# Feed-forward chunks: the order of 512-column and 256-column products on TensorE

## The chip, the cores and the metric

The kernel runs on one core of a Trainium2 chip. Its engines are TensorE (PE in the profile, with its weight loads as PEld), VectorE (DVE), ScalarE (ACT), GpSimd (POOL) and SyncE (SP, which issues nearly all DMAs here). The metric is the device time of one launch in microseconds, lower is better. Three runs of the kernel before took 1203.28, 1199.79 and 1201.71 us, median 1201.71 us.

## The reference, cut to what matters

Two decoder layers over 256 tokens of width 1024. Each layer has two feed-forward parts (SwiGLU), with a token mixer and a cross-attention between them. The change touches the feed-forward parts alone:

```python
def swiglu_ffn(x, w_gu, w_down):
    gate, up = jnp.split(x @ w_gu, 2, axis=-1)
    return (jax.nn.silu(gate) * up) @ w_down
# D_MODEL = 1024, D_FF = 2816: w_gu is 1024 x 5632, w_down 2816 x 1024, all float32
# per layer: x += 1/2 swiglu(rms_norm(x)); mixer; cross-attention; x += 1/2 swiglu(rms_norm(x))
```

So there are four feed-forward parts in the program, each with a gate-and-up product and a down product.

## The kernel before, in words

Every float32 operand is split in two float32r parts, a high part (the rounded value) and a low part (the rest). A product is then three products: high by high, high by low, low by high. The helper `weights` brings one weight tile of 128 x 1024 by DMA into one of four `raw` buffers; for the gate-and-up weights that is two DMAs of 256 KB (line 171). ScalarE casts the tile to its high part `wh` (line 175) and VectorE subtracts to get the low part `wl` (line 177). There are ten buffers each for `wh` and `wl`, and a `raw` buffer is free again when its `wl` is done.

The gate-and-up product of one feed-forward part is done in eleven chunks of 256 features. A chunk uses four weight tiles; tile i holds the rows of k = 2i and 2i + 1, the 256 gate columns and the 256 up columns. Weights are stationary here and the activations stream: `xs` holds, per k, the high part of 2 x 128 tokens and the low part of 2 x 128 tokens, four runs of 128 columns in all. A product with `wh` therefore streams 512 columns (high and low part of x, line 323) into the two halves of a PSUM bank, and a product with `wl` streams 256 columns (the high part of x alone, line 324) and adds to the first half. The helper `ws_wide` does this for one half of a chunk (g = 0 gate, g = 1 up): two banks (b), and for each bank eight k, the 512-column product and the 256-column product in turn. A chunk has 4 banks and 32 such pairs. When a bank is done, ScalarE copies its second half out (line 327) and VectorE adds the first half to it (line 328). Then come the Silu (line 416), the product with the up half (line 418) and the split of the result into two parts (lines 190 and 191, tile `big`).

In the first feed-forward part chunk 0 is done in another way (lines 305 and 182 to 184, streams of 256 columns), and chunks 1 to 10 with `ws_wide`. In the other three, chunks 0 and 1 are done by tokens (lines 182 to 184, streams of 512 columns), and chunks 2 to 10 with `ws_wide`; while chunk 2 runs, two transposes of line 397 come in between. That makes 10 + 3 x 9 = 37 wide chunks, 1184 pairs. The down product `project` follows with streams of 512 columns (lines 182 to 184).

PSUM has six rotating banks for these products. Engines work through their instructions in the order that the scheduler wrote; TensorE's order is that of the source, with the delayed pieces (`later`, `tick`) put in where their due time on the planner's clock has passed. The DMA queue is SyncE's; it issues a weight tile when a `raw` buffer is free.

Of the kernel before, what the change touches and what calls it, by code (L numbers as in the profile page):

```python
# [18 lines left out]
P = 128  # L19
S = 256  # L20
D = 1024
NK = D // P
# [16 lines left out]
def kernel(  # L39
# [33 lines left out]
    nc = tc.nc  # L73
# [18 lines left out]
    def later(delay, fn, tag=None):  # L92
        serial[0] += 1
        heapq.heappush(heap, (clock[0] + delay, serial[0], tag, fn))

    def dispatch():
        due, _, _, fn = heapq.heappop(heap)
        clock[0] = max(clock[0], due)
        busy[0] = True
        fn()  # L100
        busy[0] = False

    def tick(ns):
        clock[0] += ns
        if heap and not busy[0] and heap[0][0] <= clock[0]:
            dispatch()

    def need(tag):
        while any(e[2] == tag for e in heap):
            dispatch()  # L110

    def flush():
        while heap:
            dispatch()
# [27 lines left out]
    xs = const.tile([P, 2, 2, NK, P], F32R, name="xs")  # L142
    xh, xl = xs[:, 0], xs[:, 1]
# [3 lines left out]
    def psum():  # L147
        return mm.tile([P, 512], F32, name="mm")

    def tps():  # L150
        return tp.tile([P, 512], F32, name="tp")

    def slot(dt=F32):
        return big.tile([P, 1024], dt, name="big")

    def work(dt=F32):
        return wk.tile([P, 512], dt, name="wk")
# [4 lines left out]
    def blocks(ap, n=P):  # L162
        return ap.rearrange("p (a b) -> p a b", b=n)


    def weights(src, r=None, kept=False):
        if r is None:
            r = raw.tile([P, 1024], F32, name="raw")
        if len(src.shape) == 4:
            for g in range(2):  # L170
                nc.sync.dma_start(r.rearrange("p (k g n) -> p k g n", g=2, n=src.shape[3])[:, :, g, :], src[:, :, g, :])
        else:
            (kept_load if kept else nc.sync.dma_start)(r if len(src.shape) == 2 else blocks(r, src.shape[2]), src)
        wh = wsp.tile([P, 1024], F32R, name="wh")
        nc.scalar.copy(wh, r)  # L175
        wl = wsp.tile([P, 1024], F32R, name="wl")
        nc.vector.tensor_tensor(wl, r, f32(wh), op=ALU.subtract)  # L177
        return wh, wl

    def mm3(ps, a, b, start, stop):  # L180

        nc.tensor.matmul(ps, lhsT=a[0], rhs=b[0], start=start, stop=False)  # L182
        nc.tensor.matmul(ps, lhsT=a[0], rhs=b[1], start=False, stop=False)  # L183
        nc.tensor.matmul(ps, lhsT=a[1], rhs=b[0], start=False, stop=stop)  # L184

    def cols(w, o, n):
        return w[0][:, o:o + n], w[1][:, o:o + n]

    def split_to(dh, dl, src):
        nc.scalar.copy(dh, src)  # L190
        nc.vector.tensor_tensor(dl, src, f32(dh), op=ALU.subtract)  # L191
# [45 lines left out]
    def announce(vec, kept=False):  # L237
        upcoming["gain"] = None if vec is None else load_gain(vec, kept)
# [21 lines left out]
    def xparts(t, k):  # L260
        return xh[:, t, k, :], xl[:, t, k, :]
# [49 lines left out]
                mm3(ps[:, b * 256:(b + 1) * 256], cols(w[k // per], o, P), xboth(k), k == 0, k == NK - 1)  # L311
                tick(330)

    def ws_wide(w, g):


        part, out = work(), work()
        for b in range(2):
            ps = psum()
            for k in range(NK):  # L320
                o = (k % 2) * 512 + g * 256 + b * P
                wh, wl = cols(w[k // 2], o, P)
                nc.tensor.matmul(ps, lhsT=wh, rhs=xs[:, :, :, k, :], start=k == 0, stop=False)  # L323
                nc.tensor.matmul(ps[:, 0:256], lhsT=wl, rhs=xh[:, :, k, :], start=False, stop=k == NK - 1)  # L324
                tick(347)
            bs = slice(b * 256, (b + 1) * 256)
            nc.scalar.copy(part[:, bs], ps[:, 256:512])  # L327
            nc.vector.tensor_tensor(out[:, bs], ps[:, 0:256], part[:, bs], op=ALU.add)  # L328
        return out


    def start(load):


        et = mybir.EngineType
        with tc.manual_schedule(engines={et.Pool, et.DVE, et.Activation, et.PE}):
            upcoming["gain"] = [psum(), psum()]
            for c in range(2):
                nc.tensor.matmul(upcoming["gain"][c], lhsT=ones[0:1, 0:P], rhs=row[0:1, c * 512:(c + 1) * 512],
                                 start=True, stop=True)  # L340
            busy_ps = tps()
            for i in range(2):
                nc.tensor.matmul(busy_ps, lhsT=filler[:, 0:P], rhs=filler, start=i == 0, stop=i == 1)
            r0 = raw.tile([P, 1024], F32, name="raw")
            nc.vector.tensor_copy(r0[:, 0:1], xres[0][:, D - 1:D])
            for t in range(2):
                for c in range(2):
                    x_updated(t, c)
                clock[0] += 3000.0
            upcoming["starting"] = True  # L350
            need("x0")
            first = load(0, r0)
            need("x1")
            rest = load(1, None)
            upcoming["starting"] = False
            return first, rest

    def ffn(w_gu, w_down, next_vec, first=False):
        wv = w_gu.rearrange("(k p) n -> p k n", p=P)
        wgu = w_gu.rearrange("(k p) (g n) -> p k g n", p=P, g=2)  # L360
        hts = []

        def load_chunk(c):

            return [weights(wgu[:, 2 * i:2 * i + 2, :, c * 256:(c + 1) * 256]) for i in range(4)]

        def hslot(c):
            if c % 2 == 0:
                hts.append((slot(F32R), slot(F32R)))
            return [blocks(h[:, (c % 2) * 512:(c % 2) * 512 + 512], 256) for h in hts[c // 2]]  # L370

        ws = hs = None
        if first:
            f, r = start(lambda i, r: [weights(wv[:, 0:4, 0:256], r, kept=True)] if i == 0 else
                         [weights(wv[:, 4 * (n % 2):4 * (n % 2) + 4, (n // 2) * DFF:(n // 2) * DFF + 256],
                                 kept=True)
                          for n in range(1, 4)])
            ws = [[[f[0], r[0]], r[1:]]]
        else:
            need("x0")  # L380
            ws = [load_chunk(0), load_chunk(1)]
            hs = [hslot(0), hslot(1)]
        for t in range(2):
            need(f"x{t}")
            for c in range(0 if first else 2):
                ps = psum()
                for k in range(NK):
                    mm3(ps, xparts(t, k), cols(ws[c][k // 2], (k % 2) * 512, 512), k == 0, k == NK - 1)
                    tick(650)
                h = work()  # L390
                nc.scalar.activation(h[:, 0:256], ps[:, 0:256], AF.Silu)
                nc.vector.tensor_tensor(h[:, 256:512], ps[:, 256:512], h[:, 0:256], op=ALU.mult)

                def to_features(t=t, c=c, h=h):
                    pst = tps()
                    for b in range(2):
                        nc.tensor.transpose(pst[:, b * P:(b + 1) * P], h[:, 256 + b * P:256 + (b + 1) * P], ident)
                    split_to(hs[c][0][:, :, t * P:(t + 1) * P], hs[c][1][:, :, t * P:(t + 1) * P],
                             blocks(pst[:, 0:256]))
                later(LAG['silu'], to_features)  # L400
        if not first:
            announce(next_vec)
        for c in range(0 if first else 2, NF // 2):
            w = ws[0] if first and c == 0 else load_chunk(c)
            if first and c == 2:
                announce(next_vec, kept=True)
            if first and c == 0:
                pg = psum()
                ws_blocks(pg, w[0], 0, 4, by_pass=True)
                pu = psum()  # L410
                ws_blocks(pu, w[1], 0, 4)
            else:
                pg = ws_wide(w, 0)
                pu = ws_wide(w, 1)
            s = work()
            nc.scalar.activation(s, pg, AF.Silu)
            h = work()
            nc.vector.tensor_tensor(h, pu, s, op=ALU.mult)
            dh, dl = hslot(c)
            split_to(dh, dl, blocks(h, 256))  # L420
        flush()

        def hparts(t, k):
            o = (k % 4) * 256 + t * P
            return hts[k // 4][0][:, o:o + P], hts[k // 4][1][:, o:o + P]

        project(lambda k: w_down[k * P:(k + 1) * P, :], hparts, add_to_x(0.5), nk=NF)
# [626 lines left out]
```

## Time and profile before

| what | value |
|---|---|
| median of three runs | 1201.71 us (1199.79 to 1203.28) |
| profiled execution, its own time | 1202.92 us |
| span in the profile | 1201.2 us |
| PE busy | 1189.3 us (99%) |
| PEld busy | 998.7 us (83%) |
| DVE busy | 775.1 us (65%) |
| ACT busy | 646.5 us (54%) |
| DMA queue, share of 16 engines' span | 55.4% |

The span runs from the first to the last instruction in the profile; the execution's own time is 1.7 us longer. The duration of a matmul in the profile is longer than the distance to the next one's start, because matmuls overlap; what a product costs in a stream is read from the starts of neighbouring rows, not from its duration.

### The profile page before, as it was taken

How to read it: one execution, taken by the hardware profiler on the slowest of the kernel's cores; microseconds unless marked ns; L12 is line 12 of the kernel's file. 1: busy time of each engine (PE TensorE's matmuls, PEld its weight loads, DVE VectorE, ACT ScalarE, POOL GpSimd, SP SyncE). 2: the span in 40 equal slices, each digit the busy share in tenths (PEclk: the TensorE clock that was granted, in tenths of full speed). 3: DMA queues.
4: the chain of work that ended last, by engine and by line, in shares of the span. 5: the costliest groups of instructions: out<-in, count | busy, mean ns of one | idle time of the engine just before them, and what ended most of it. 6: DMA issues, size and time to landing. Idle time of an engine off the chain costs nothing.

```text
span 1201.2 us, 16964 instructions
## 1 busy us (share of the span) xinstructions
PE 1189.3 (99%) x6320; PEld 998.7 (83%) x6320; DVE 775.1 (65%) x1026; ACT 646.5 (54%) x1080; POOL 63.9 (5%) x123
## 2 busy tenths in 40 slices
PE   8999999999999999999999999999999999999998
PEld 7888888986788888888888888888777888888887
DVE  6766645696777676665375765376786676667651
ACT  6656534665565466555265564265764564655540
POOL 1000000200110000000000000032000100000000
PEclk9999999999999999999999999999999999999999
DMA  8865674731454485666376657445753645665560
GB/s 253 255 195 172 218 223 131 258 105 53 145 167 144 153 266 172 191 209 210 108 250 189 193 181 274 141 158 167 230 169 121 210 143 160 202 205 188 182 192 35
DMA packets 136756, 216.70 MB, mean 180 GB/s; under 512 B 10337, under 2 KB 104161, under 8 KB 136674
## 3 DMA queue, kind: packets, MB, share of 16 engines
q1 hardware_dynamic: 136674, 215.63, 55.4%
q8 instruction: 49, 0.80, 0.3%
q14 instruction: 33, 0.27, 0.1%
HBM read 214.54 MB, written 1.05 MB: 179 GB/s over the span
## 4 chain that ended last, share of the span: by engine, by line
PE 93%; DVE 3%; DMA 2%; ACT 1%; issue 1%; POOL 0%; SPq 0%; ACTq 0%; POOLq 0%; DVEq 0%
PE mm L323 23%; PE mm L182 17%; PE mm L184 17%; PE mm L183 17%; PE mm L324 12%; PE tp L212 3%; PE mm L496 1%; DVE wl L177 1%; DMA raw<-in_xa_w_o_dram 1%; DMA raw<-in_ffn_w_gu_dram 1%; ACT wh L175 1%; PE mm L305 1%; PE mm L841 1%; DVE big L191 0%; PE mm L705 0%
## 5 line engine op out<-in xcount | busy, mean ns | idle before, releaser
L177 DVE TENSOR_TENSOR wl<-raw,wh 128x1024 fp32r<-128x1024 f32 x386 | 463.9, 1220 | 145.4 <-ACT wh L175 142.5
L175 ACT CAST wh<-raw 128x1024 fp32r<-128x1024 f32 x386 | 394.3, 1051 | 156.9 <-PE mm L184 78.7
L323 PE MATMUL mm<-xs,wh 128*128 128x512 f32 x1184 | 413.7, 394 | 0.0
L324 PE MATMUL mm<-xs,wl 128*128 128x256 f32 x1184 | 331.8, 280 | 0.0
L323 PEld LDWEIGHTS mm<-xs,wh 128*128 128x128 f32 x1184 | 221.7, 187 | 50.3
L324 PEld LDWEIGHTS mm<-xs,wl 128*128 128x128 f32 x1184 | 223.8, 189 | 0.0
L182 PE MATMUL mm<-wh,big 128*128 128x512 f32 x480 | 191.3, 399 | 0.3 <-DVE wk L713 0.3
L184 PE MATMUL mm<-wh,big 128*128 128x512 f32 x480 | 188.4, 392 | 0.0
L183 PE MATMUL mm<-wl,big 128*128 128x512 f32 x480 | 188.2, 392 | 0.0
L182 PE MATMUL mm<-wh,xs 128*128 128x512 f32 (+1 forms) x432 | 171.7, 398 | 0.0
L184 PE MATMUL mm<-wh,xs 128*128 128x512 f32 (+1 forms) x432 | 167.1, 387 | 0.0
L183 PE MATMUL mm<-wl,xs 128*128 128x512 f32 (+1 forms) x432 | 167.0, 386 | 0.0
L327 ACT COPY wk<-mm 128x256 f32<-128x256 f32 x148 | 55.0, 372 | 147.1 <-PE mm L324 146.7
L328 DVE TENSOR_TENSOR wk<-mm,wk 128x256 f32<-128x256 f32 x148 | 62.1, 421 | 94.7 <-ACT wk L327 94.7
L182 PEld LDWEIGHTS mm<-wh,big 128*128 128x128 f32 x480 | 90.5, 188 | 20.3 <-issue 2.4
L184 PEld LDWEIGHTS mm<-wh,big 128*128 128x128 f32 x480 | 90.4, 188 | 19.3 <-issue 0.3
L183 PEld LDWEIGHTS mm<-wl,big 128*128 128x128 f32 x480 | 90.6, 189 | 17.4 <-issue 0.2
L184 PEld LDWEIGHTS mm<-wh,xs 128*128 128x128 f32 x432 | 81.1, 188 | 16.9 <-issue 0.2
L182 PEld LDWEIGHTS mm<-wh,xs 128*128 128x128 f32 x432 | 81.3, 188 | 15.0 <-issue 0.5
L183 PEld LDWEIGHTS mm<-wl,xs 128*128 128x128 f32 x432 | 81.4, 188 | 14.5 <-issue 0.2
L212 PE MATMUL tp<-ident,wk 128*128 128x128 f32 x352 | 52.9, 274 | 2.4 <-DVE wk L452 0.8
L212 PEld LDWEIGHTS tp<-ident,wk 128*128 128x128 f32 x352 | 42.1, 140 | 14.2 <-issue 2.3
(148 smaller groups left out, 921.6 us busy)
## 6 DMA issues: line engine op xcount, KB each, us to landing
raw<-in_ffn_w_gu_dram SPq DMA_DIRECT2D x344, 256.0 KB, 4.2
raw<-in_ffn_w_down_dram SPq DMA_DIRECT2D x88, 512.0 KB, 4.5
raw<-in_xa_w_kv_dram SPq DMA_DIRECT2D x32, 512.0 KB, 5.4
raw<-in_od_w_in_dram SPq DMA_DIRECT2D x24, 512.0 KB, 4.5
raw<-in_ev_w_in_dram SPq DMA_DIRECT2D x18, 512.0 KB, 4.7
raw<-in_xa_w_q_dram SPq DMA_DIRECT2D x16, 512.0 KB, 4.2
raw<-in_xa_w_o_dram SPq DMA_DIRECT2D x16, 512.0 KB, 4.4
raw<-in_ev_w_out_dram SPq DMA_DIRECT2D x8, 512.0 KB, 4.1
```

Of the source, the lines that this page charges most:

```text
L175: nc.scalar.copy(wh, r)
L177: nc.vector.tensor_tensor(wl, r, f32(wh), op=ALU.subtract)
L182: nc.tensor.matmul(ps, lhsT=a[0], rhs=b[0], start=start, stop=False)
L183: nc.tensor.matmul(ps, lhsT=a[0], rhs=b[1], start=False, stop=False)
L184: nc.tensor.matmul(ps, lhsT=a[1], rhs=b[0], start=False, stop=stop)
L212: nc.tensor.transpose(ps[:, b * P:(b + 1) * P], src[:, b * P:(b + 1) * P], ident)
L305: nc.tensor.matmul(ps[:, b * 256:(b + 1) * 256], lhsT=w[k // per][x][:, o:o + P], rhs=xboth(k)[y], start=i == 0 and k == 0, stop=i == 2 an ...
L323: nc.tensor.matmul(ps, lhsT=wh, rhs=xs[:, :, :, k, :], start=k == 0, stop=False)
L324: nc.tensor.matmul(ps[:, 0:256], lhsT=wl, rhs=xh[:, :, k, :], start=False, stop=k == NK - 1)
L327: nc.scalar.copy(part[:, bs], ps[:, 256:512])
L328: nc.vector.tensor_tensor(out[:, bs], ps[:, 0:256], part[:, bs], op=ALU.add)
L496: nc.tensor.matmul(dst(h)[rows], lhsT=lhs(h), rhs=rhs(h), start=first, stop=last)
```

## The change

`ws_wide`, called twice per chunk, becomes `ws_chunk`, called once. It does the 32 products of 512 columns of a chunk first, over four banks, and then the 32 products of 256 columns over the same four banks. The instructions are the same in number and kind; the copies and adds that empty a bank now follow that bank's last 256-column product, in the second part of the chunk.

```diff
-    def ws_wide(w, g):
-        part, out = work(), work()
-        for b in range(2):
-            ps = psum()
+    def ws_chunk(w):
+        pair, outs = [(g, b) for g in range(2) for b in range(2)], []
+        banks = []
+        for g, b in pair:
+            banks.append(psum())
             for k in range(NK):
                 o = (k % 2) * 512 + g * 256 + b * P
-                wh, wl = cols(w[k // 2], o, P)
-                nc.tensor.matmul(ps, lhsT=wh, rhs=xs[:, :, :, k, :], start=k == 0, stop=False)
-                nc.tensor.matmul(ps[:, 0:256], lhsT=wl, rhs=xh[:, :, k, :], start=False, stop=k == NK - 1)
-                tick(347)
+                nc.tensor.matmul(banks[-1], lhsT=w[k // 2][0][:, o:o + P], rhs=xs[:, :, :, k, :],
+                                 start=k == 0, stop=False)
+                tick(227)
+        for (g, b), ps in zip(pair, banks):
+            for k in range(NK):
+                o = (k % 2) * 512 + g * 256 + b * P
+                nc.tensor.matmul(ps[:, 0:256], lhsT=w[k // 2][1][:, o:o + P], rhs=xh[:, :, k, :],
+                                 start=False, stop=k == NK - 1)
+                tick(120)
+            if b == 0:
+                part, out = work(), work()
+                outs.append(out)
             bs = slice(b * 256, (b + 1) * 256)
             nc.scalar.copy(part[:, bs], ps[:, 256:512])
             nc.vector.tensor_tensor(out[:, bs], ps[:, 0:256], part[:, bs], op=ALU.add)
-        return out
+        return outs
...
-                pg = ws_wide(w, 0)
-                pu = ws_wide(w, 1)
+                pg, pu = ws_chunk(w)
```

On TensorE, where chunk 1 of the first feed-forward part begins, this stood before (`mm` is a PSUM bank, `xs` the activations, lines 182 to 184 the end of chunk 0):

```order
58 L182 MATMUL mm<-xs,wh 128x256
59 L183 MATMUL mm<-xs,wh 128x256
60 L184 MATMUL mm<-xs,wl 128x256
61 L323 MATMUL mm<-xs,wh 128x512
62 L324 MATMUL mm<-xs,wl 128x256
63 L323 MATMUL mm<-xs,wh 128x512
```

and so on, 32 times in turn per chunk. Now this stands there, with the whole of chunk 1 in its last two rows:

```order
58 L182 MATMUL mm<-xs,wh 128x256
59 L183 MATMUL mm<-xs,wh 128x256
60 L184 MATMUL mm<-xs,wl 128x256
61 L324 MATMUL mm<-xs,wh 128x512 x32
62 L330 MATMUL mm<-xs,wl 128x256 x32
```

Products of one size now stand 32 in a row and all four banks of the chunk stay open until its last third. No other instruction of TensorE has moved.

On VectorE, in chunk 2 of the same part, this stood before (`wl` is a low part being made for a later chunk, line 328 the add that empties a bank, line 418 the product with the up half, line 191 the split; numbers tell buffers apart):

```order
37 L191 TENSOR_TENSOR big_304<-wk_417,big_303 128x512
38 L328 TENSOR_TENSOR wk_452<-mm_453,wk_451 128x256
39 L328 TENSOR_TENSOR wk_452<-mm_472,wk_451 128x256
40 L328 TENSOR_TENSOR wk_492<-mm_493,wk_491 128x256
41 L177 TENSOR_TENSOR wl_672<-raw_667,wh_670 128x1024
42 L177 TENSOR_TENSOR wl_679<-raw_674,wh_677 128x1024
43 L328 TENSOR_TENSOR wk_492<-mm_512,wk_491 128x256
44 L177 TENSOR_TENSOR wl_774<-raw_769,wh_772 128x1024
45 L418 TENSOR_TENSOR wk_533<-wk_492,wk_531 128x512
```

and this stands there now:

```order
38 L338 TENSOR_TENSOR wk_496<-mm_451,wk_495 128x256
39 L338 TENSOR_TENSOR wk_496<-mm_460,wk_495 128x256
40 L177 TENSOR_TENSOR wl_672<-raw_667,wh_670 128x1024
41 L338 TENSOR_TENSOR wk_518<-mm_469,wk_517 128x256
42 L338 TENSOR_TENSOR wk_518<-mm_478,wk_517 128x256
43 L177 TENSOR_TENSOR wl_679<-raw_674,wh_677 128x1024
44 L427 TENSOR_TENSOR wk_533<-wk_518,wk_531 128x512
45 L177 TENSOR_TENSOR wl_774<-raw_769,wh_772 128x1024
46 L191 TENSOR_TENSOR big_536<-wk_533,big_535 128x512
47 L177 TENSOR_TENSOR wl_781<-raw_776,wh_779 128x1024
```

The four adds of a chunk now stand together, with one low part between the second and the third, and the other three low parts of the chunk's time behind them. ScalarE's order has moved in the same way: three casts, the copies of banks 0 and 1, one cast, the copies of banks 2 and 3, the Silu.

## Rows read from the trace of the kernel before

**Rows 1.** Page: busy time, share and instructions; granted clock in 40 slices.
```profile
PE 1189.3 (99%) x6320; PEld 998.7 (83%) x6320; DVE 775.1 (65%) x1026; ACT 646.5 (54%) x1080; POOL 63.9 (5%) x123
...
PEclk9999999999999999999999999999999999999999
```

**Rows 2.** Page: the chain that ended last, by engine and by line.
```profile
PE 93%; DVE 3%; DMA 2%; ACT 1%; issue 1%; POOL 0%; SPq 0%; ACTq 0%; POOLq 0%; DVEq 0%
PE mm L323 23%; PE mm L182 17%; PE mm L184 17%; PE mm L183 17%; PE mm L324 12%; PE tp L212 3%; PE mm L496 1%; DVE wl L177 1%; DMA raw<-in_xa_w_o_dram 1%; DMA raw<-in_ffn_w_gu_dram 1%; ACT wh L175 1%; PE mm L305 1%; PE mm L841 1%; DVE big L191 0%; PE mm L705 0%
```

**Rows 3.** Page: costliest groups (xcount, busy us, mean ns, idle before).
```profile
L177 DVE TENSOR_TENSOR wl<-raw,wh 128x1024 fp32r<-128x1024 f32 x386 | 463.9, 1220 | 145.4 <-ACT wh L175 142.5
L175 ACT CAST wh<-raw 128x1024 fp32r<-128x1024 f32 x386 | 394.3, 1051 | 156.9 <-PE mm L184 78.7
L323 PE MATMUL mm<-xs,wh 128*128 128x512 f32 x1184 | 413.7, 394 | 0.0
L324 PE MATMUL mm<-xs,wl 128*128 128x256 f32 x1184 | 331.8, 280 | 0.0
...
L327 ACT COPY wk<-mm 128x256 f32<-128x256 f32 x148 | 55.0, 372 | 147.1 <-PE mm L324 146.7
L328 DVE TENSOR_TENSOR wk<-mm,wk 128x256 f32<-128x256 f32 x148 | 62.1, 421 | 94.7 <-ACT wk L327 94.7
```

**Rows 4.** Windows, line 323 alone: us, PE busy (x), PEld busy (x), PEclk, DMA share, GB/s.
```profile
26.27:139.33 113.06, 113.06 (x320) 60.01 (x320) 1.00 0.65 208
448.60:543.20 94.60, 94.59 (x273) 51.03 (x273) 1.00 0.59 188
632.90:727.50 94.60, 94.50 (x274) 51.05 (x273) 1.00 0.59 187
1042.70:1137.30 94.60, 94.53 (x273) 51.05 (x273) 1.00 0.58 187
```

**Rows 5.** Windows, PE alone: us, PE busy (x), PEclk, DMA share, GB/s.
```profile
20.75:26.15 5.40, 5.40 (x47) 1.00 0.94 299
1142.07:1179.47 37.40, 37.40 (x167) 1.00 0.46 150
443.08:448.47 5.39, 5.39 (x33) 1.00 0.83 266
```

**Rows 6.** Timeline, PE, 512 to 256 to 512 columns (start us, us).
```profile
199.89 0.39 PE L184 MATMUL mm<-wh,big 128*128 128x512 f32 x1
200.12 0.28 PE L182 MATMUL mm<-wh,xs 128*128 128x256 f32 x1
...
202.99 0.40 PE L182 MATMUL mm<-wh,xs 128*128 128x512 f32 x1
203.22 0.40 PE L183 MATMUL mm<-wl,xs 128*128 128x512 f32 x1
...
204.15 0.39 PE L184 MATMUL mm<-wh,xs 128*128 128x512 f32 x1
```

**Rows 7.** Timeline, PE, a wide chunk of the second feed-forward part.
```profile
507.63 0.39 PE L323 MATMUL mm<-xs,wh 128*128 128x512 f32 x1
507.86 0.28 PE L324 MATMUL mm<-xs,wl 128*128 128x256 f32 x1
507.98 0.39 PE L323 MATMUL mm<-xs,wh 128*128 128x512 f32 x1
```

**Rows 8.** Timeline, one chunk: ACT, then DVE, with idle time before.
```profile
80.98 1.98 ACT L175 CAST wh<-raw 128x1024 fp32r<-128x1024 f32 x2
...
88.66 0.37 ACT L327 COPY wk<-mm 128x256 f32<-128x256 f32 x1 [1.52 <-PE mm L324]
91.53 0.37 ACT L327 COPY wk<-mm 128x256 f32<-128x256 f32 x1 [2.50 <-PE mm L324]
...
82.05 2.36 DVE L177 TENSOR_TENSOR wl<-raw,wh 128x1024 fp32r<-128x1024 f32 x2 [1.04 <-ACT wh L175]
85.80 0.69 DVE L418 TENSOR_TENSOR wk<-wk 128x512 f32<-128x512 f32 x1
...
87.87 0.68 DVE L191 TENSOR_TENSOR big<-wk,big 128x512 fp32r<-128x512 f32 x1
```

**Rows 9.** Issue of one weight tile on SP; DMA issues: xcount, KB each, us to landing.
```profile
72.00 0.88 SPq L171 DMA_DIRECT2D raw<-in_ffn_w_gu_dram  x2
...
raw<-in_ffn_w_gu_dram SPq DMA_DIRECT2D x344, 256.0 KB, 4.2
...
raw<-in_ffn_w_gu_dram SPq DMA_DIRECT2D x4, 512.0 KB, 6.9
```

## The prediction

> **What bounds the kernel now.** I read the page from the top. TensorE is busy 99% of the span, at the full clock (2.4 GHz, the granted share is at 9 or more tenths) in every slice [rows 1], and the chain of waits that ended last is 93% TensorE, 35% in the two lines that the change reorders [rows 2]. So the wide chunks are paid for at the pace at which TensorE starts products, and the only direct question is what 32 wide and 32 narrow products cost in turn and what they cost in two blocks. The mean durations of the groups (394 and 280 ns, [rows 3]) don't tell, since matmuls overlap. I took stretches and divided them by the number of starts.
>
> In turn, the kernel before shows two paces for the same instructions. In the first feed-forward part 320 pairs took 113.06 us, 353.3 ns a pair; in the other three, 273 pairs took 94.60 us, 346.5 ns (one window cuts so that it counts 274) [rows 4]. Among the latter I count only what follows the last transpose of line 397. The 15 pairs of chunk 2 before it took 5.39 us [rows 5]; at 346.5 ns they would take 5.20, so 0.19 us is lost there. A start right after transposes is late once; that part I put at 0.09 us and leave it as it is, and 0.10 is the slow pace (15 x 6.7 ns).
>
> In blocks, the nearest streams of one size are: 256 columns alone, the same activations and weights of the same kind, 45 steps in 5.40 us, 120.0 ns; 512 columns alone, in the down product, 165 steps in 37.40 us, 226.7 ns [rows 5]. Their sum is 346.7 ns. So the quick pace in turn is already the sum of the two streams, and the slow one is 6.7 ns above it. What the change can win is the slow pace, where it rules: 320 pairs of the first part, 45 in the others.
>
> **The change part by part.** TensorE's instructions keep their number: 1184 wide and 1184 narrow products with their weight loads.
>
> The blocks. A chunk is 32 x 226.7 + 32 x 120.0 ns = 11.09 us.
>
> The seams. A place that goes from wide to 24 narrow and back stands in the trace: from the last wide start at 199.89 to the sixth wide start after the narrow ones, at 204.15, are 4.26 us [rows 6]. The streams' paces give 0.227 + 24 x 0.120 + 5 x 0.2267 = 4.24. So two seams cost 0.02 us; the five wide starts behind the narrow stream come 0.232 us apart, near the slow pace, and then the pace is quick again. A chunk is thus 11.11 us.
>
> The sum. First part: 10 chunks x (32 x 0.3533 = 11.306, less 11.113) = 1.93 us less. Other parts: 27 chunks x (11.113 less 32 x 0.3465 = 11.088) = 0.68 more, and 3 x 0.10 less. In all 1.55 us less, on the profiled execution's 1202.92 us: 1201.4 us. That execution lies 1.2 us above the median of the runs, and I carry the saving over to the median: 1200.2 us.
>
> In the Trainium skill, "TensorE: Matmul & The Clock Gate", section Back-to-back issue gap, a warm product alone is given as its columns over 2.4 GHz and about 2.5 ns, here 216 and 109 ns. By it each size has one price, whatever its neighbour, and the change would be worth nothing. The two paces of one instruction pair in this trace (353.3 and 346.5 ns) are both above the 325 that it gives, and they differ: the trace does not agree.
>
> The emptying of banks. Four copies (0.372 us) and four adds (0.421 us) per chunk stay, but come at its end. A bank is needed again after the two spare ones: bank 0 is full 32 x 0.2267 + 8 x 0.12 = 8.2 us into the chunk and is needed 16 x 0.2267 = 3.6 us into the next, so 6.5 us later, of which copy and add take 0.8. That leaves 5.7 us in which waits on ScalarE are free. Before, ScalarE sat idle in front of these copies for 147 us in all [rows 3], 1.5 and 2.5 us at a time [rows 8]; it waited for TensorE, not the other way. I cost the move at nothing under that cover.
>
> The weights. The low parts of a chunk are freed only in its last 0.8 us now, and VectorE makes the new ones in the order one, then three behind the Silu of the chunk, with 0.69 us of other work between. The new round is: the last low part frees a raw buffer; SP's two issues (0.88 us, the second about 0.4 in) and 4.2 us to landing [rows 9], 4.6; the cast 1.05; copies of banks 2 and 3, 0.74; the add 0.42; then low part, product, low part, split, low part, 3 x 1.22 + 2 x 0.69 = 5.04 [rows 3, 8]. That is 11.85, less some 0.1 where neighbours on an engine overlap (two casts take 1.98 us and two low parts 2.36, [rows 8]), six times, so about 11.3 us against a chunk of 11.11. The round would slip 0.2 us per chunk, 2 us in ten chunks, out of 5.7. It stays hidden on these numbers, without much to spare. Products themselves have their weights a chunk or more ahead.
>
> **The rivals.**
>
> *Emptying of banks falls behind (slower).* The same round decides from a landing about 0.4 us over the 4.2, since a slip of 0.6 per chunk uses the 5.7 us in ten chunks. From then on TensorE waits at the third bank of each chunk. With landings 0.6 us longer the slip is 0.8, the cover lasts 7 chunks, and 3 chunks of the first part and 2 of each other pay: 9 x 0.8 = 7.2 us, less 1.55: 1207.4. For it: there are landings of 6.9 us in this trace, if of tiles in one piece [rows 9], and at the start of the first part the DMAs run at 208 GB/s over the whole part. Against it: the issues will come further apart (about 1.9 us) than they do now.
>
> *The wide block stays slow (slower).* The wide products read four runs of 128 columns, those of the down product one run of 512; no stream of the former alone is in the trace. If the five slow starts of [rows 6] go on through all 32, a chunk is 32 x (0.3533 - 0.120) + 3.84 = 11.306: nothing is won in the first part, and 27 x 0.218 less 0.3 = 5.6 us are lost: 1207.3. Against it: the quick pace in turn has room for no more than 226.7 ns for such a product, if the narrow one takes its 120.
>
> *Narrow products have been cheap in turn.* The starts in turn are 0.23 us from wide to narrow and 0.12 back [rows 7]. If a wide product really takes 0.230 and the narrow one less than 0.120 because its weight load is hidden under a wide one, blocks cost 350 ns a pair: 1.06 us less in the first part and 27 x 0.112 - 0.3 = 2.7 more: 1203.4. The Trainium skill, in the same page's section LDWEIGHTS, puts a load of 128 columns at their number over 1.2 GHz, 107 ns, as long as 256 streamed columns; no run here times a load alone.
>
> *The slow pace is no matter of order.* Then the first part stays at 353 ns a pair or the runs change between paces by themselves; the three runs differ by 3.5 us as it is. Nothing changes: 1201.7. If, the other way, the runs without profile have the slow pace in all parts, the gain is 37 x 0.193 = 7.1 us: 1194.6; the profiled one, above the median, has it in one part of four.
>
> **How the numbers follow.** My forecast has 0.50, the banks 0.18, the wide block 0.10, the narrow products 0.08, no change 0.09, the larger gain 0.05. What a measurement of this kernel can tell from no change is about 0.3%, 3.6 us. The forecast, the narrow products and no change lie within it; Of the forecast I give 0.07 to a saving over that bound, should the seams be cheaper and the slow pace more common than one profile shows; of the banks' case 0.03 to a loss below it. Faster 0.05 + 0.07 = 0.12, slower 0.15 + 0.10 = 0.25, same 0.63. The likeliest case alone reaches from 1198.5 to 1202. The range takes in both slower cases and a part of the larger gain: 1197 to 1208.5.
>
> **What would show it.** In the profile after: wide products in the chunks start 226 to 228 ns apart but for some five at the head of a block, narrow ones 120; a chunk takes 11.1 us in all four parts, and the first part's ten chunks end about 1.9 us earlier after their start. Rows of TensorE at the head of the third bank have no idle time in front, and ScalarE still waits for TensorE at the copies. I am wrong if gaps stand in front of the third wide bank, growing from chunk to chunk, if the wide blocks hold 233 ns, or if the first part has not changed its pace.

## The result: slower by 1.4%

The changed kernel took 1218.33 us (median of 4 runs, 1217.26 to 1222.16), the kernel before 1201.58 us beside it: a ratio of 1.0143, 95% interval 1.0122 to 1.0164. The forecast was 1200.2 us. The profiled execution of the changed kernel took 1219.17 us, its span is 1217.1 us, 15.9 more than before. In its profile the 512-column products are line 324, the 256-column ones line 330, the copies that empty a bank line 337 and the adds line 338.

The page of the changed kernel, busy times, then the chain that ended last by engine and by line; they answer to [rows 1, 2]:

```profile
PE 1193.1 (98%) x6320; PEld 999.6 (82%) x6320; DVE 768.8 (63%) x1026; ACT 645.8 (53%) x1080; POOL 63.9 (5%) x123
...
PE 62%; DVE 15%; DMA 13%; issue 6%; ACT 3%; SPq 1%; POOL 0%; ACTq 0%; DVEq 0%; POOLq 0%
PE mm L182 18%; PE mm L184 17%; PE mm L183 17%; DMA raw<-in_ffn_w_gu_dram 8%; DVE wl L177 7%; DMA raw<-in_ffn_w_down_dram 5%; DVE wk L338 4%; PE mm L324 3%; PE tp L212 3%; DVE wk L427 2%; ACT wh L175 1%; PE mm L505 1%; ACT wk L337 1%; PE mm
```

The share of busy time has hardly moved. The chain has: TensorE fell from 93% to 62% of it, and where lines 323 and 324 held 35%, the weights' DMA, the low parts and the adds now stand between TensorE's pieces.

The groups of the same page, which answer to [rows 3] (times, busy us and mean ns, idle before and what ended it), and the waits of the whole program (us, times, longest):

```profile
L175 ACT CAST wh<-raw 128x1024 fp32r<-128x1024 f32 x386 | 401.4, 1052 | 264.9 <-DMA raw<-in_ffn_w_gu_dram 96.2
...
L338 DVE TENSOR_TENSOR wk<-mm,wk 128x256 f32<-128x256 f32 x148 | 55.9, 417 | 161.7 <-ACT wk L337 161.6
...
raw<-in_ffn_w_gu_dram SPq DMA_DIRECT2D x344, 256.0 KB, 4.0
```

```profile
DVE wk L338 <- ACT wk L337: 161.6, 40, 4.9
...
PE mm L182 <- DVE wk L338: 9.0, 4, 2.5
```

Before, ScalarE's idle time stood in front of the copies and TensorE ended it (147 us). Now no such row is left for the copies. More idle time stands in front of the casts (264.9 us against 156.9), and the gate-and-up DMAs end 96.2 us of it (29.4 before); the adds wait up to 4.9 us for a copy, and four times, once per feed-forward part, TensorE waits 2.1 to 2.5 us for an add at the head of the down product.

The pace is as forecast. Windows of line 324 alone over the first wide chunk, then of line 330 in it (us, PE busy, PEld busy, clock, DMA share, GB/s); they answer to [rows 4]:

```profile
24.16:31.42 7.26, 7.26 (x32) 5.82 (x32) 1.00 0.84 263
...
31.43:35.26 3.83, 3.82 (x32) 3.78 (x31) 1.00 1.09 365
```

A wide product costs 7.26/32 = 0.227 us, a narrow one 0.120. What was not forecast stands in whole chunks. Windows of TensorE from the start of one wide chunk to the next (us, PE busy; the difference is idle time, as far as it outlasts the tail of the product before), first part, then the second:

```profile
46.39:57.50 11.11, 11.11 (x67) 1.00 0.52 161
68.65:80.65 12.00, 11.45 (x67) 1.00 0.55 167
80.65:92.59 11.94, 11.40 (x67) 1.00 0.60 189
92.59:103.95 11.36, 11.36 (x66) 1.00 0.59 167
103.95:116.11 12.16, 11.42 (x67) 1.00 0.61 195
116.11:127.35 11.24, 11.24 (x66) 1.00 0.53 169
...
513.55:525.22 11.67, 11.42 (x67) 1.00 0.61 187
```

The first four chunks take the 11.11 us of the forecast, the next five 58.70 us, 11.74 on the mean. TensorE waits there at the third bank, behind 16 of the 32 wide products; in the first of these chunks:

```profile
73.01 3.96 PE L324 MATMUL mm<-xs,wh 128*128 128x512 f32 x16 [0.55 <-DVE wk L338]
```

The two traces, laid side by side at the same instructions of TensorE, give the whole difference:

| where | us, after less before |
|---|---|
| up to the first wide chunk (loading of x and chunk 0, which the change doesn't touch) | -2.11 |
| wide chunks, pace and seams: first part -1.93, others +0.33 | -1.60 |
| wide chunks, waits at the third bank: parts one to four 3.77, 1.34, 1.06, 0 | +6.17 |
| down product, wait at its third bank: 2.36, 2.70, 2.48, 2.35 | +9.89 |
| down product of parts one and two, half clock behind that wait: 1.74, 1.76 | +3.50 |
| everything else | +0.04 |
| sum | +15.89 |

The first row stands ahead of all that the change touches: TensorE came to its full pace later in the trace of before, where four 256-column products of chunk 0 still take 1.22 us at 13.5 us; in that of after four take 0.74 at 12.5. Without this row the change costs 18.0 us here. "Everything else" is -0.43 and +0.47 between the parts.

**The round that is longer than a chunk.** ScalarE, then VectorE in a chunk of the first part (start us, us, idle before):

```profile
106.68 1.05 ACT L175 CAST wh<-raw 128x1024 fp32r<-128x1024 f32 x1 [1.76 <-DMA raw<-in_ffn_w_gu_dram]
107.63 0.64 ACT L337 COPY wk<-mm 128x256 f32<-128x256 f32 x2
108.16 1.06 ACT L175 CAST wh<-raw 128x1024 fp32r<-128x1024 f32 x1
109.11 0.66 ACT L337 COPY wk<-mm 128x256 f32<-128x256 f32 x2
...
101.93 1.22 DVE L177 TENSOR_TENSOR wl<-raw,wh 128x1024 fp32r<-128x1024 f32 x1
108.03 0.76 DVE L338 TENSOR_TENSOR wk<-mm,wk 128x256 f32<-128x256 f32 x2 [4.88 <-ACT wk L337]
...
109.83 0.75 DVE L338 TENSOR_TENSOR wk<-mm,wk 128x256 f32<-128x256 f32 x2
110.50 1.21 DVE L177 TENSOR_TENSOR wl<-raw,wh 128x1024 fp32r<-128x1024 f32 x1
...
113.97 1.22 DVE L177 TENSOR_TENSOR wl<-raw,wh 128x1024 fp32r<-128x1024 f32 x1
```

The copies at 107.63 and 109.11 have no wait of their own: they run as soon as the cast ahead of them is over. Each cast needs a DMA, the DMA a raw buffer, and the buffer a low part; for the cast at 108.16 it is the low part that ended at 103.15. This low part stands on VectorE behind the adds of the last chunk, which waited for that chunk's copies. So the copies are a link of a closed round: here from 103.15 to the end of the last low part at 115.19, 12.04 us; over the five chunks that it sets, 11.74 on the mean. The first copy of a chunk starts 11.5, 13.1, 13.8, 14.6, 15.5 us after the chunk's first product in the first five chunks, until TensorE itself is held up; in the last part it slips from 9.3 to 13.8 over nine chunks. Where nothing holds it up it starts at 8.4 (the next run); so in the first part 3.1 us of the cover were gone in the first chunk already.

TensorE at the head of the down product, first part:

```profile
139.07 0.40 PE L182 MATMUL mm<-wh,big 128*128 128x512 f32 x1
...
140.23 0.39 PE L184 MATMUL mm<-wh,big 128*128 128x512 f32 x1
142.81 0.50 PE L182 MATMUL mm<-wh,big 128*128 128x512 f32 x1 [2.18 <-DVE wk L338]
...
144.33 0.63 PE L184 MATMUL mm<-wh,big 128*128 128x512 f32 x1
144.76 0.63 PE L182 MATMUL mm<-wh,big 128*128 128x512 f32 x1
...
741.99 0.50 PE L182 MATMUL mm<-wh,big 128*128 128x512 f32 x1 [2.20 <-DVE wk L338]
```

The last row is the same wait in part three. There a bank takes only three products at first, so the third bank is due after six, 1.36 us, and not after sixteen. Windows of TensorE behind that place in parts one to four (granted clock behind the PE column):

```profile
144.30:147.30 3.00, 3.00 (x9) 0.52 0.63 175
...
554.20:557.20 3.00, 3.00 (x9) 0.57 0.72 190
742.00:745.00 3.00, 3.00 (x13) 1.00 0.21 34
1154.70:1157.70 3.00, 3.00 (x13) 1.00 0.11 30
```

In parts one and two the granted clock went to about half, the 1.2 GHz level, and products started 0.43 us apart in place of 0.23.

### The profile page after: what moved, and what is told of

The parts are those of the page before. It is cut to its first block, busy times and chain, and to the rows that moved or that the text cites. A ratio compares the mean times of both kernels' runs of the same rounds, so it can differ in the third digit from the quotient of the medians.

```text
span 1217.1 us, 17029 instructions
## 1 busy us (share of the span) xinstructions
PE 1193.1 (98%) x6320; PEld 999.6 (82%) x6320; DVE 768.8 (63%) x1026; ACT 645.8 (53%) x1080; POOL 63.9 (5%) x123
## 4 chain that ended last, share of the span: by engine, by line
PE 62%; DVE 15%; DMA 13%; issue 6%; ACT 3%; SPq 1%; POOL 0%; ACTq 0%; DVEq 0%; POOLq 0%
PE mm L182 18%; PE mm L184 17%; PE mm L183 17%; DMA raw<-in_ffn_w_gu_dram 8%; DVE wl L177 7%; DMA raw<-in_ffn_w_down_dram 5%; DVE wk L338 4%; PE mm L324 3%; PE tp L212 3%; DVE wk L427 2%; ACT wh L175 1%; PE mm L505 1%; ACT wk L337 1%; PE mm L330 1%; SPq L171 1%
## 5 line engine op out<-in xcount | busy, mean ns | idle before, releaser
L175 ACT CAST wh<-raw 128x1024 fp32r<-128x1024 f32 x386 | 401.4, 1052 | 264.9 <-DMA raw<-in_ffn_w_gu_dram 96.2
L324 PE MATMUL mm<-xs,wh 128*128 128x512 f32 x1184 | 279.6, 392 | 3.0 <-DVE wk L338 2.8
L324 PEld LDWEIGHTS mm<-xs,wh 128*128 128x128 f32 x1184 | 218.7, 188 | 51.2 <-DVE wk L338 7.7
L338 DVE TENSOR_TENSOR wk<-mm,wk 128x256 f32<-128x256 f32 x148 | 55.9, 417 | 161.7 <-ACT wk L337 161.6
L330 PEld LDWEIGHTS mm<-xs,wl 128*128 128x128 f32 x1184 | 146.9, 192 | 2.9
L330 PE MATMUL mm<-xs,wl 128*128 128x256 f32 x1184 | 147.8, 283 | 0.0
L190 ACT CAST big<-wk 128x512 fp32r<-128x512 f32 x38 | 23.6, 622 | 72.8 <-DVE wk L427 72.8
```

The lines of the kernel that those rows point to most:

```text
L324: nc.tensor.matmul(banks[-1], lhsT=w[k // 2][0][:, o:o + P], rhs=xs[:, :, :, k, :], start=k == 0, stop=False)
L330: nc.tensor.matmul(ps[:, 0:256], lhsT=w[k // 2][1][:, o:o + P], rhs=xh[:, :, k, :], start=False, stop=k == NK - 1)
```

## The experiments

Theory A is the round above: copies wait in ScalarE's queue behind casts that wait for DMAs, with four raw buffers the round is longer than a chunk, and the banks come free late. Its rivals: the block order keeps the banks open too long whatever ScalarE does (B), the DMAs can't deliver in this order (C), each cast ahead of a copy costs a landing however many buffers there are (D).

**Copies first.** TensorE's order stays; the weights of the chunk after next are written behind the chunk, and their casts are pinned there.

```diff
-        nc.scalar.copy(wh, r)
+        cast = nc.scalar.copy(wh, r)
+        if behind:
+            tc.keep_in_program_order(cast)
...
                 pg, pu = ws_chunk(w)
+                if c + 2 < nc_:
+                    ahead[c + 2] = load_chunk(c + 2, behind=True)
```

> TensorE's order, tiles and buffers are those of the changed kernel; only the casts of the chunk after next are pinned behind the four copies of the running chunk in ScalarE's order (before: one of them stood between the copies of banks 1 and 2, and one for a later chunk ahead of the copy of bank 0). Theory A (copies wait in ScalarE's queue behind casts that wait for their DMA, and this round is longer than a chunk): no copy waits for a DMA any more, no gap stands in front of third wide banks or of the down product's third bank, time 1199 to 1203 us. Rival B (the block order itself leaves the banks open too long, whatever ScalarE does): the 161 us of idle time at the adds and the gaps stay, 1214 to 1219 us. Rival C (the weights cannot come in time in this order, the DMAs set the pace): the gaps move to the wide products, which wait for wh or wl, over 1206 us.

Measured: 1199.58 us, before 1202.22, ratio 0.9972 (0.9959 to 0.9985). ScalarE in one chunk (here 339 are the copies, 332 the narrow products), then two chunks of TensorE, of the first and the last part:

```profile
110.60 0.37 ACT L339 COPY wk<-mm 128x256 f32<-128x256 f32 x1 [3.60 <-PE mm L332]
111.50 0.37 ACT L339 COPY wk<-mm 128x256 f32<-128x256 f32 x1 [0.53 <-PE mm L332]
...
113.69 2.94 ACT L175 CAST wh<-raw 128x1024 fp32r<-128x1024 f32 x3
```

```profile
57.66:68.77 11.11, 11.11 (x66) 1.00 0.58 184
1077.67:1088.78 11.11, 11.11 (x66) 1.00 0.62 188
```

A copy waits for TensorE again and the casts run when the copies are through. No gap is left in the chunks or at the down product. Against the trace of before, the first part's chunks are 1.94 us shorter and the others' 0.16, 0.11 and 0.11 longer; 1.93 and 0.38 in sum had been forecast. B and C fall. On VectorE the low part between the adds has moved behind them too; the run with five raw buffers, below, keeps one there and has no gaps in its chunks either. The kernel is also faster than both others.

**Shorter blocks.** Blocks of two banks, then of one bank, in place of four; the two loops over k stand inside as they did:

```diff
-        for g, b in pair:
-            banks.append(psum())
...
-        for (g, b), ps in zip(pair, banks):
+        for g in range(2):
+            banks = []
+            for b in range(2):
+                banks.append(psum())
...
+            for b in range(2):
+                ps = banks[b]
```

```diff
+        for g in range(2):
+            part, out = work(), work()
+            outs.append(out)
+            for b in range(2):
+                ps = psum()
```

> Blocks of two banks: 16 wide products, then 16 narrow ones, for the gate half, then the same for the up half. The scheduler then writes three casts between the two pairs of copies. Theory A: copies and casts stand spread over the chunk as before, so a copy waits at most for one landing that has had half a chunk; a bank is open for 5.5 us in place of 8.2; few or no gaps, chunk 11.13 us (two more seams of 0.02 us in total), 1199 to 1203 us. Rival B (block order leaves banks open too long): gaps smaller but there, 1206 to 1212 us. Rival C (DMAs set the pace): 1210 to 1219 us, as the bytes per chunk are the same.

> Blocks of one bank: 8 wide products, then 8 narrow ones, four times per chunk. ScalarE's order is then nearly that of the kernel before. Theory A: no gaps, and only the seams (four per chunk, about 0.01 to 0.06 us each) are added to 11.09 us: 1199 to 1202 us, in the first feed-forward part 1.5 us less than before. Rival C (DMAs): gaps as in the changed kernel, over 1210 us. If the slow pace of the first part (353.3 ns a pair) comes back although pairs no longer alternate, 1202 to 1204 us.

Measured: 1200.86 us, ratio 0.9984 (0.9973 to 0.9995), and 1203.14 us, 1.0006 (0.9997 to 1.0016). A chunk of each, two banks, then one:

```profile
57.95:69.08 11.13, 11.13 (x66) 1.00 0.74 216
```

```profile
60.53:71.70 11.17, 11.17 (x66) 1.00 0.63 189
```

Two, four and eight seams give 11.11, 11.13 and 11.17 us: 0.01 us a seam on 11.09. Neither has a gap, as A had it. The second missed its range by a little though its mechanism held. Its further seams are worth 37 x 0.04 = 1.5 of the 2.3 us between the two medians; its profiled execution also reached the first wide chunk 2.5 us later than that with two banks, before anything that differs.

**Seven banks.** The transposes give up one of their two banks:

```diff
-    mm = ctx.enter_context(tc.tile_pool(name="mm", bufs=6, space=PSUM))
-    tp = ctx.enter_context(tc.tile_pool(name="tp", bufs=2, space=PSUM))
+    mm = ctx.enter_context(tc.tile_pool(name="mm", bufs=7, space=PSUM))
+    tp = ctx.enter_context(tc.tile_pool(name="tp", bufs=1, space=PSUM))
```

> The changed kernel with seven rotating PSUM banks for the products and one, not two, for the transposes: each bank is due one bank (1.81 us) later. Theory A: the copies slip by 0.6 to 0.7 us in each chunk whatever the cover, so the cover is used up some three chunks later: the gaps inside the first part fall from 3.8 to 1 us, those of parts two and three (1.35, 1.06) go, but the head of the down product, where the cover grows by 0.68 us only while the slip goes on, still waits 2 to 3 us in each part: 1211 to 1216 us. Rival B (cover short by a fixed size): all gaps go, 1200 to 1204 us. The single bank for transposes may cost some us in mixers and attention, which is told apart by where the difference arises.

Measured: 1241.42 us, ratio 1.033 (1.0306 to 1.0354). The first gap in the chunks comes one chunk later (chunk 6 of the program's count, the window below), and the gaps of the first part sum to 3.0 us, where A had put them three chunks later and at 1 us; those of parts two and three are gone, as A had it. At the down product's head the wait has moved to the fourth bank. It is 3.35, 3.38, 1.73 and 2.91 us, longer than with six banks in all parts but the third:

```profile
79.93:92.39 12.46, 11.41 (x67) 1.00 0.57 168
```

```profile
144.04 0.80 PE L182 MATMUL mm<-wh,big 128*128 128x512 f32 x1 [3.35 <-DVE wk L338]
```

With half clock behind three of the four (granted 0.70 to 0.77 over 3 us) this costs 5.0, 5.2, 2.0 and 4.5 us. So more cover lets the copies slip further, as A says, and B falls again. The total missed its range because the stretches between the feed-forward parts cost 20 us more than in the kernel before (6.9 between parts one and two, 12.6 between three and four). That this is the single bank of the transposes is likely, but no run shows it alone. The Trainium skill, "Perfetto Trace Analysis", section Optimization Strategy, says that one gap repeating on the engine that should be full can mean too little SBUF or PSUM for the next tile. The traces agree for SBUF and not for PSUM: TensorE waits for a PSUM bank, but a seventh bank did not end the gaps, and a fifth raw buffer, which lies in SBUF, did (the next runs).

**More raw buffers.** The next three belong together: five raw buffers, paid for with two work buffers; those work buffers alone; six raw buffers, paid for with nine buffers each for the parts.

```diff
-    raw = ctx.enter_context(tc.tile_pool(name="raw", bufs=4))
+    raw = ctx.enter_context(tc.tile_pool(name="raw", bufs=5))
...
-    wk = ctx.enter_context(tc.tile_pool(name="wk", bufs=10))
+    wk = ctx.enter_context(tc.tile_pool(name="wk", bufs=8))
```

```diff
-    raw = ctx.enter_context(tc.tile_pool(name="raw", bufs=4))
-    wsp = ctx.enter_context(tc.tile_pool(name="wsp", bufs=10))
+    raw = ctx.enter_context(tc.tile_pool(name="raw", bufs=6))
+    wsp = ctx.enter_context(tc.tile_pool(name="wsp", bufs=9))
```

> The changed kernel with five raw buffers in place of four, and eight work buffers in place of ten to make room (the next run shows what these cost alone). The scheduler then puts one cast, still for a chunk two or three ahead, between the copies of banks 0 and 1, so copies still stand behind casts that wait for a landing. Theory A (the copies are a link of a closed round: low part frees a raw buffer, DMA, cast, copies, adds, low part; 12.04 us measured against a chunk of 11.11, so 0.6 to 0.7 us of slip per chunk): with five buffers a round may take 5/4 of a chunk, 13.9 us, so the copies no longer slip, no gap inside the parts, and little or none at the down product: 1199 to 1205 us. Rival D (each cast ahead of a copy holds it up by one landing, however many buffers there are): 1212 to 1219 us.

> Control for the run with five raw buffers: the changed kernel with eight work buffers in place of ten, four raw buffers as they were; ScalarE's order in the chunks is that of the changed kernel. Theory A and rival D both: like the changed kernel, 1216 to 1222 us. If it comes out near 1200, the work buffers and not the raw ones matter.

> The changed kernel with six raw buffers and nine, not ten, buffers each for the high and the low parts. Again casts stand ahead of the copies of banks 0 and 1. Theory A: a round may take 6/4 of a chunk, 16.7 us; no slip, no gaps, 1199 to 1204 us, no better than with five. Rival D: 1212 to 1219 us. Nine buffers for parts may cost some us at the changes between stages, which would show there and not in the chunks.

Measured: 1199.35 us with five (0.9975, 0.9960 to 0.9990), 1222.21 for the control (1.0167, 1.0133 to 1.0200; 0.2 us above its range, with waits at the third bank and at the down products as in the changed kernel), 1202.95 with six (0.9998, 0.9983 to 1.0013). With five, the waits of the adds, ScalarE in a chunk of the third part, and TensorE's only wait at a bank, at the head of the first down product:

```profile
DVE wk L338 <- ACT wk L337: 144.7, 73, 4.4
```

```profile
665.20 3.13 ACT L175 CAST wh<-raw 128x1024 fp32r<-128x1024 f32 x3 [1.60 <-PE mm L324]
668.24 0.36 ACT L337 COPY wk<-mm 128x256 f32<-128x256 f32 x1
669.06 1.05 ACT L175 CAST wh<-raw 128x1024 fp32r<-128x1024 f32 x1 [0.46 <-DMA raw<-in_ffn_w_gu_dram]
670.02 0.64 ACT L337 COPY wk<-mm 128x256 f32<-128x256 f32 x2
...
139.31 0.50 PE L182 MATMUL mm<-wh,big 128*128 128x512 f32 x1 [1.07 <-DVE wk L338]
```

Copies still stand behind casts: the first one behind three, which wait here for TensorE to be done with a high part, and the other three behind a fourth, which waits for a DMA. The adds still wait for copies 144.7 us in all (161.6 in the changed kernel). But the slip has all but gone: the first copy of a chunk stays between 9.0 and 9.8 us in parts two to four and goes from 9.9 to at most 11.8 in the first, and the chunks take 11.11 but for those with transposes. D falls. The idle time at the adds does not tell the slow kernel from the quick one; the length of the round against the chunk does. The scheduler's order has changed with the buffers, by the cast between the copies of banks 0 and 1; no run has the fifth buffer alone. With six buffers the chunks have no gap either; why its median lies 3 us above that with five was not followed up, its profiled span (1197.6 us) does not show it.

**What the gain over the kernel before is.** The kernel before with the same pinned casts:

```diff
                 pu = ws_wide(w, 1)
+                if c + 2 < nc_:
+                    ahead[c + 2] = load_chunk(c + 2, behind=True)
```

> The kernel before (products in turn) with the casts pinned behind the copies as in the run that pinned them in the changed kernel. It tells what of that run's 0.28% over the kernel before is the block order and what the pinned casts. If the block order gives it by taking the first part's slow pace (353.3 ns a pair) away: this kernel stays at the time of the kernel before, 1200.5 to 1203.5 us, with a pace of 346.5 or 353.3 ns in turn in its parts. If the pinning gives it: 1198 to 1200 us.

Measured: 1200.93 us, 0.9987 (0.9972 to 1.0001). Wide products of nine chunks of the first part and of seven of the second (the counts take in neighbours cut by the window's ends):

```profile
25.94:127.70 101.76, 101.76 (x288) 54.17 (x289) 1.00 0.65 206
454.36:532.02 77.66, 77.66 (x226) 41.90 (x225) 1.00 0.62 191
```

101.76/288 is 353.3 ns a pair, 77.66/224 is 346.7: both paces are there as in [rows 4]. The pinning takes nothing off the chunks; the block order does.

**Where the slow pace comes from.** In the kernel before, one bank as a block, and one pair of transposes that nothing needs, each in a kernel of its own, at the start of chunk 4 of the first part; the third kernel pins the transposes:

```diff
+            if block and b == 0:
+                for part_ in range(2):
+                    for k in range(NK):
...
-                pg = ws_wide(w, 0)
+                pg = ws_wide(w, 0, block=first and c == 4)
```

```diff
+                if first and c == 4:
+                    pst = tps()
+                    for b in range(2):
+                        nc.tensor.transpose(pst[:, b * P:(b + 1) * P], ident, ident)
+                    nc.vector.tensor_copy(work()[:, 0:256], pst[:, 0:256])
```

```diff
-                        nc.tensor.transpose(pst[:, b * P:(b + 1) * P], ident, ident)
+                        tc.keep_in_program_order(nc.tensor.transpose(pst[:, b * P:(b + 1) * P], ident, ident))
```

> The kernel before, with one bank of the whole program (first bank of chunk 4 of the first feed-forward part) as 8 wide products and then 8 narrow ones; all else in turn. It asks where the slow pace of the first part (353.3 ns a pair against 346.7 in the others) comes from. Theory P (the pace is kept by the alternating stream itself and set anew when the stream is broken): chunks 1 to 3 at 353.3 ns a pair, the rest of the part after the block at 346.7, about 1.4 us less in the part (6.75 chunks of 32 pairs times 6.6 ns). Rival Q (the pace belongs to the first part, for its DMAs or its operands): 353.3 before and after the block. The block order gains 1.94 us in that part either way; only P would make this gain one of breaking the stream.

> The kernel before, with two transposes of 128 columns put in front of chunk 4 of the first feed-forward part (and one VectorE copy of their result, which nothing uses); all else in turn. The other three parts have two transposes in their chunk 2 and run at 346.7 ns a pair behind them. Theory P: chunks 1 to 3 at 353.3, chunks 4 to 10 at 346.7, about 1.5 us less less the cost of the transposes (some 0.3 us). Rival Q: 353.3 throughout.

> As the run before it with one pair of transposes, which the scheduler had moved to 6.4 us, far ahead of the chunks; here they are pinned between chunks 3 and 4 of the first part. One bank in blocks had not changed the pace behind it. If transposes set the pace (in the other parts 346.7 ns a pair stand only behind them): chunks 1 to 3 at 353.3 ns a pair, chunks 4 to 10 at 346.7, some 1.5 us less in the part. If the pace belongs to the first part: 353.3 throughout.

The block: 1202.5 us, 0.999 (0.997 to 1.001). Two chunks ahead of it and five behind it (line 333 is the wide product there):

```profile
25.95:48.56 22.61, 22.61 (x64) 12.03 (x65) 1.00 0.90 279
71.14:127.67 56.53, 56.53 (x161) 30.07 (x161) 1.00 0.58 186
```

353.3 ns a pair on both sides (22.61/64, 56.53/160). The first run with transposes (1202.24 us, 1.0001) told nothing, as they ran at 6.4 us, before all chunks. With the transposes pinned in place (1201.02 us, 0.9998, 0.9983 to 1.0013), two chunks ahead and five behind:

```profile
24.48:47.09 22.61, 22.61 (x65) 12.03 (x65) 1.00 0.89 274
69.73:125.20 55.47, 55.47 (x162) 29.92 (x161) 1.00 0.59 190
```

353.3 ns ahead of them, 55.47/160 = 346.7 behind, to the end of the part. That is also the sequence at the transposes of line 397 in the other parts of the kernel before [rows 4, 5]. But the second part of the kernel with one block, where its source is that of the kernel before, has it the other way round; 13 steps ahead of those transposes and seven chunks behind them:

```profile
444.04:448.55 4.51, 4.51 (x15) 2.43 (x14) 1.00 0.91 282
455.13:534.27 79.14, 79.14 (x226) 42.09 (x225) 1.00 0.60 186
```

4.51/13 = 347 ns ahead, 79.14/224 = 353.3 behind. So in these traces two transposes change the pace, one way or the other. The part does not fix it, and a break by a block of 8 and 8 products did not change it.

## Why the prediction was wrong

**The pace and the seams: right.** 11.11 us per chunk in every part, -1.93 and +0.38 us: that was the forecast's sum, and the copies-first run measured -1.94 and +0.38. Of the kernels in this block order without gaps in the chunks two lie where the forecast put the time (1199.58 and 1199.35 us), the one with six raw buffers 3 us higher. The wide block did not stay slow, and the narrow products were not cheaper in turn: both rivals fall. Of the rival in which the pace is no matter of order a part holds: which parts run slowly in turn is not fixed by the source, as the kernel with one block shows, so the gain may differ from one execution to the next.

**"I cost the move at nothing under that cover": the step that failed.** The cover was taken from a ScalarE that waits for TensorE [rows 3]. But ScalarE takes its instructions in order, and in the new order, which the rows of the change showed, three casts for a chunk two or three ahead stand in front of the first copy and one in the middle. What waits then is not ScalarE's spare time but the DMA of that cast. The prediction worked out the round with the copies in it and still called the copies covered. Moving the copies ahead of the casts, with TensorE's order in place, gave 18.8 us back (1218.33 to 1199.58 in medians).

**The round, a term mis-sized.** Forecast 11.3 us, measured 11.74 on the mean and 12.04 in the chunk shown. By terms of that chunk: freed buffer to the start of its cast 108.16 - 103.15 = 5.01 (forecast 4.6); cast, copies and adds to the next low part 110.50 - 108.16 = 2.34 (2.21); the last leg with three low parts 115.19 - 110.50 = 4.69 (5.04). Against its terms the last leg came out 0.35 shorter, where 0.6 had been deducted for overlaps in all; the middle one, which holds a pair of adds and not one, came out 0.13 longer, and the way to the cast 0.4 longer. The median landing was no longer than before (4.0 us, [rows 9] has 4.2). So the slip was 0.6 us per chunk and not 0.2: the very value at which the prediction's own rival decides. That rival priced the gaps inside the parts at 7.2 us; they were 6.17.

**The due time at the down product, missed.** The cover was counted for the next chunk (16 products, 3.6 us) and not for the next user of the bank, which needs it after 6. The waits there cost 9.89 us in four parts, and struck the last part too, where no gap stood inside the chunks.

**The clock, missed.** 3.5 us behind two of the four waits. The Trainium skill, "TensorE: Matmul & The Clock Gate", section A second HAM failure mode: psum-queue depth-cycling, says that pauses between groups of products as the banks go round can cost the clock's full level. Two waits of 2.18 and 2.54 us here agree; one of 2.20 us in part three and that of part four kept the full clock.

The forecast's mark of being wrong, gaps in front of the third wide bank that grow from chunk to chunk, is what came, but for the growth: once TensorE waits, the round sets the chunk.

## What to carry to other kernels

When the order of one engine's work is changed, read on every engine that empties buffers what now stands ahead of the emptying, and what that waits for: an engine's idle time is cover only if its queue is not blocked. Compare a closed round (buffer freed, DMA, cast, copy, add, buffer freed) with the period of the loop: a few tenths too long use up a fixed cover turn by turn. Here the copies moved out of the round cured it, and so did a further buffer of the round's scarce kind (with the order that the scheduler then chose); a bank more of cover did not. Look for the first consumer after the loop, since it may want a buffer sooner than the next turn.

## What the runs showed of the hardware

The same alternating pairs of 512- and 256-column products run at 353.3 or at 346.7 ns a pair, at full clock. One stream that began at the slow pace kept it for ten chunks, through a block of 8 and 8 products; one went over to the quick pace behind two transposes of 128 columns and kept that; one went from the quick pace to the slow one behind two such transposes and kept that. Why was not settled. In blocks the pace is the quick sum, 226.9 and 119.7 ns, with 0.01 us a seam.

The same wait of TensorE of about 2.2 us was followed by half clock in one part and by full clock in another; in the control with eight work buffers one of 2.46 us was followed by half clock and one of 2.56 us by the full one. What tells them apart stays open.
